# A two-layer decoder trunk: the residual stream kept with channels on the partitions from the first output projection on

## The chip, the cores and the metric

The kernel runs on one core of a Trainium2 chip. The metric is the time of one execution on the device in microseconds (us). The engines are TensorE (PE: matrix products; PEld: its weight loads), VectorE (DVE), ScalarE (ACT), GpSimd (POOL) and SyncE (SP, which issues nearly all DMAs here). Each engine works through its own instructions in order; semaphores tie the engines together.

## The reference

The input x has 512 tokens of 1024 channels. Two layers follow each other. The attention branches are not touched by the change, and stand here as one call each.

```python
for i in range(2):
    h = rms_norm(x, norm_gain[i])                    # over the 1024 channels
    y = (even_layer, odd_layer)[i](h, ...)           # h @ w_in, four kinds of attention, gates, then @ w_out
    x = x + y
    gate = sigmoid(rms_norm(x, ple_norm_gain[i]) @ w_ple_gate[i])
    x = x + (p[i] @ w_ple_proj[i]) * gate            # per-layer embedding
return x
```

`even_layer` has indexer-selected attention and a sliding window, `odd_layer` dilated and differential attention. Both end in `concat(...) @ w_out`, 1024 x 1024.

## The kernel before

**Products.** Everything is float32. Each operand of a projection is split into a rounded part and a rest (`hilo`: ScalarE writes the rounded part, VectorE subtracts), and a product is made of three passes (`PASSES`) of 128 x 128 x 512. `AT` holds the activations of the running projection with channels on the partitions: 8 channel tiles of 128 channels x 512 tokens, both parts. `w2` tiles (eight buffers) hold the split weights. `proj_tok` (L406) makes a token-major result: a 128-token slice of `AT` is the stationary operand, 512 columns of weights are streamed, and each of the four token tiles fills a PSUM bank (`mm_bank`, four of them). With order "kt" the weight tiles are the outer loop and all banks finish together; with "tok" one token tile is finished after the other. `proj_gate` (L441) does it the other way: 128 columns of weights stand still, 512 tokens are streamed, and the result has channels on the partitions. The trace writes the streamed operand first: `mm<-w,AT` is `proj_tok`, `mm<-AT,w` is `proj_gate`.

**The residual stream.** `X` is two tiles, one for each half of the channels, with 128 tokens on the partitions and 4 token tiles x 512 channels along them. `reload_x` (L740) brings x back before the output projection. `out_half` (L729) multiplies one branch's half of the concatenation by `w_out`, first for the lower 512 output channels ("kt"), then for the upper 512 ("kt" or "tok"); `add_x` adds a bank to `X`. `norm` (L510) then takes the four token tiles: `turn` transposes 4 blocks of 128 x 128 on TensorE for each half and splits them into `AT` (`swap` puts the lower half's channels in the upper half of `AT`, since the other half is still read); `norm_scale` sums the squares of a token by ScalarE's accumulator, adds the two halves on VectorE and takes the power -0.5 on GpSimd, one column per token tile. The scale of the norm is applied after the projection, as a number per partition (per token). `ple` (L744) is the gate of the per-layer embedding: two halves of 512 channels, each `proj_tok` with order "tok" and 96 products; `evac` applies tanh with the scale on ScalarE, and two VectorE steps build the new `X`, which is written to `out` or to `xkept`. In the very last half the last token tile is made in two pieces of 256 columns (`cut`). `ple_products` (L707) makes the product of p and `w_ple_proj` ahead of time. Three norms use `turn`: those of the two embeddings and that of layer 1. `scale_rows` (L494) makes the scales available along the free dimension, for `proj_gate`, by two DMAs through DRAM.

**The order.** The program records all instructions with an estimated duration, and `Program.order` plays them through a list scheduler: on each engine the ready instruction with the lowest rank goes next, the rank being its place in the program less a lead from the table `LEADS`, one entry for each call of a marked function. The resulting order of each engine is fixed. In the trace every instruction has line L278, where they are issued, so that groups are told apart by their tiles (`sk` is the bank that `turn` fills, `tk` that of the heads' and probabilities' turns).

Of the kernel before, what the change touches and what calls it, by code (L numbers as in the profile page):

```python
# [21 lines left out]
P = 128  # L22
# [9 lines left out]
    "att": (-392, -476, -265, 55, 575, -382, 44, 15, -6, -149, -341, -446, -4, -57, 63, -14, 2, 2, -287, 388, 0, 0,  # L32
# [7 lines left out]
    "idx": (-5, -2, 0),  # L40
    "mm": (15, 0, 153, 0, 10, -336, -84, 2, 8, 4, 0, -30, 30, -5, 88, -12, -304, 0, 41, 13, 136, -25, 206, -141, -135,
         -6, -996, -1930, -2303, -10383),
    "norm": (-3, -2, 0, -170, 60, -38, 0, -13, 142, 15, 0, -227, 0, -49, 15, -1, 0, 0, -396, -7, 21, 0, 0, -1844),
    "rows": (0, 898),
    "ss": (-64, 0, 0, 340, 576, 4, -39, 1269, 0, 0, -74, 119, 196, 55, 333, 112, -4, 45, -250, -182, 70, 0, 0, 1, 14,
         -119, 0, 74, 0, 1, 0, -88),
    "tab": (279, 13, -4, 0, -137, -2),
    "top": (193, -101, -908, -1349, 180, 58, -8, -21, -2, 3, -1659, -1846),
    "w": (-57, 169, 413, -21, 0, -44, -172, 0, 3, 0, -2, 1, -44, 74, -2, -20, -89, 234, 3, 68, -363, 0, 0, -80, -19,
         0, -19, 0, -854, -1336),  # L50
    "x": (2, 0),
    "y": (825, 483, 0, -2, -20, 0, 0, -16, 32, 4, 0, 202, 1, -123, -517, -335),
    None: 62,
# [26 lines left out]
class Program:  # L80
# [49 lines left out]
    def _price(self, engine, method, reads, writes):  # L130
# [22 lines left out]
        return 218 / 128 * n  # L153
# [128 lines left out]
def tile_trunk(ctx: ExitStack, tc: tile.TileContext, a: dict, out: bass.AP):  # L282
# [122 lines left out]
    @nc.part("mm")  # L405
    def proj_tok(pieces_n, evac, tiles=range(NT), order="kt", act=None, swap=0, cut=False, first=False):  # L406
        pieces, n = pieces_n
        act = [AT[:, :, kt, :] for kt in range(NK)] if act is None else act
        banks = {}
        last = len(pieces) - 1  # L410

        def mms(t, i, c0=0, c1=n, passes=range(3)):
            kt, w2 = pieces[i]
            for c in passes:
                xa, wa = PASSES[c]
                nc.tensor.matmul(banks[t][:, c0:c1], act[kt ^ (4 * swap)][:, xa, t * P:(t + 1) * P], w2[:, wa, c0:c1],
                                 start=(i == 0 and c == 0), stop=(i == last and c == 2))
        if order == "kt":
# [12 lines left out]
        else:  # L431
            for t in tiles:
                halves = ((0, 256), (256, 512)) if cut and t == NT - 1 else ((0, n),)
                for c0, c1 in halves:
                    banks[t] = mm_bank()
                    for i in range(last + 1):
                        mms(t, i, c0, c1)
                    evacuate(evac, t, banks[t], *((c0, c1) if cut else ()))

    @nc.part("mm")  # L440
    def proj_gate(pieces_n, y0, done, rsb):  # L441
# [3 lines left out]
        for i, (kt, w2) in enumerate(pieces):  # L445
            for m in range(4):
                for c, (xa, wa) in enumerate(PASSES):
                    nc.tensor.matmul(banks[m], w2[:, wa, m * P:(m + 1) * P], AT[:, xa, kt, :],
# [34 lines left out]
    def norm_scale(t, rs, times=1.0):  # L483
# [5 lines left out]
        if times != 1.0:  # L489
            nc.vector.tensor_scalar(out=e, in0=e, scalar1=times ** -2, scalar2=None, op0=ALU.mult)  # L490
# [11 lines left out]
    def turn(t, half, to):  # L502
        b = s_bank()
        for i in range(4):
            nc.tensor.transpose(b[:, i * P:(i + 1) * P], X[half][:, t, i * P:(i + 1) * P], ident)
        hs = slice(to * 4, to * 4 + 4)
        bv = b.rearrange("p (k n) -> p k n", k=4)
        hilo(AT[:, 0, hs, t * P:(t + 1) * P], AT[:, 1, hs, t * P:(t + 1) * P], bv)

    def norm(times=1.0, swap=0):  # L510
        rs = sb.tile([P, NT], F32, name=uid("rsn"), tag="rsn", bufs=2)
        for t in range(NT):
            for half in range(2):
                turn(t, half, half ^ swap)
            norm_scale(t, rs, times)
        return rs
# [190 lines left out]
    def ple_products(layer, homes=None):  # L707
        pT, _ = weights([(a["pT"][layer], T)], range(2))
        halves = []
        for c in range(2):  # L710
# [10 lines left out]
            proj_tok(weights([(a["w_ple_proj"][layer][:, c * 512:(c + 1) * 512], 512)], range(2)), evac,  # L721
                     act=[w2 for _, w2 in pT])
# [6 lines left out]
    def out_half(wout, y0, order):  # L729
        for c in range(2):  # L730
# [4 lines left out]
            proj_tok(w, add_x(c), order="kt" if c == 0 else order)  # L735
# [8 lines left out]
    def ple(layer, pws, rs, last, swap):  # L744
        for c in range(2):
# [6 lines left out]
            def evac(t, bank, c0=0, c1=512, c=c, pw=pw):  # L752
                th = tmp()[:, c0:c1]
                nc.scalar.activation(out=th, in_=bank[:, c0:c1], func=AF.Tanh, scale=rs[:, t:t + 1])
# [4 lines left out]
                nc.sync.dma_start(out=out[0, t * P:(t + 1) * P, c * 512 + c0:c * 512 + c1] if last else xkept[c][:, t, :], in_=xs)  # L759
            proj_tok(w, evac, order="tok", swap=swap, cut=last and c == 1)  # L760
# [190 lines left out]
    proj_tok(weights(ocols("ck"), range(NK), 2), head_evac(ckT, (tab_ck[:, 0], tab_ck[:, 1]), rs1), order="tok")  # L951
# [11 lines left out]
    proj_tok(weights(ocols("cv"), range(NK), 2), cv_evac)  # L963
# [78 lines left out]
    rows1 = scale_rows(rs1)  # L1042
# [4 lines left out]
    proj_tok(wcq, head_evac(cqT, (tab_cq[:, 0], tab_cq[:, 1]), rs1))  # L1047
# [3 lines left out]
    proj_gate(wdg, 4, 0, rows1)  # L1051
# [4 lines left out]
    proj_tok(wdk, head_evac(dkT, (tab_dk[:, 0], tab_dk[:, 1]), rs1))  # L1056
    wdq = weights(ocols("dq"), range(NK), 2)
    dqT = heads()
    proj_tok(wdq, head_evac(dqT, (tab_dq[:, 0], tab_dq[:, 1]), rs1))
    dV = slot([P, NT, 512])  # L1060
    proj_tok(weights(ocols("dv"), range(NK), 2), dv_evac)
# [4 lines left out]
    proj_gate(wcg, 0, 4, rows1)  # L1066
# [6 lines left out]
    ple(1, pw1, norm(0.5), True, 0)  # L1073
# [56 lines left out]
```

## Time and profile before

| | |
|---|---|
| median of three timed runs | 676.76 us (676.32 to 677.66) |
| the profiled execution | 677.39 us |
| its span from first to last instruction | 675.6 us |
| TensorE busy | 668.0 us, 3494 products |
| VectorE, ScalarE, GpSimd busy | 513.7, 415.4, 68.7 us |

All numbers of the profile are of the one profiled execution. The busy time of an engine counts each moment once, but the matrix products overlap each other, so that the mean time of one is longer than the distance from one to the next. Each digit of a line of tenths is a fortieth of the span, here 16.9 us.

### The profile page before, as it was taken

What the parts mean: (1) busy time and instruction counts of PE and PEld (TensorE: products, weight loads), DVE (VectorE), ACT (ScalarE), POOL (GpSimd) and SP (SyncE); (2) the same over time, 40 slices, a digit from 0 to 9 for tenths busy, and PEclk for the clock granted to TensorE, in tenths of its full rate; (3) what the DMA queues carried; (4) which work ended last, traced back from release to release, by engine and by line L of the source; (5) the groups of instructions that cost most, each with busy time, mean ns of one, the idle gap of its engine ahead of it and who ended that gap; (6) DMA issues with size and microseconds to landing.
All of it is one profiled execution on the core that took longest, in us unless ns stands there. A gap on an engine that the chain in (4) does not pass through costs nothing.

```text
span 675.6 us, 10378 instructions
## 1 busy us (share of the span) xinstructions
PE 668.0 (99%) x3494; PEld 543.9 (81%) x3494; DVE 513.7 (76%) x1225; ACT 415.4 (61%) x957; POOL 68.7 (10%) x55
## 2 busy tenths in 40 slices
PE   8999999999999999999999999999999999999997
PEld 5888888888988888887778877777887777888886
DVE  6699999999999646464795298989869698655443
ACT  6765678999889725355554365766637476564341
POOL 0120132000100000000230040003031000100100
PEclk9999999999999999999999999999999999999999
DMA  9855146653131521253353322123213034132222
GB/s 333 299 144 153 63 126 168 183 148 141 48 111 49 185 79 54 71 183 101 87 156 99 94 62 79 48 63 94 86 40 97 29 114 136 48 111 63 93 79 78
DMA packets 49621, 74.23 MB, mean 110 GB/s; under 512 B 5920, under 2 KB 18592, under 8 KB 49312
## 3 DMA queue, kind: packets, MB, share of 16 engines
q1 hardware_dynamic: 49424, 73.56, 35.3%
q8 instruction: 27, 0.44, 0.3%
q14 instruction: 26, 0.21, 0.1%
q10 hardware_dynamic: 144, 0.02, 0.0%
HBM read 61.49 MB, written 6.30 MB: 100 GB/s over the span
## 4 chain that ended last, share of the span: by engine, by line
PE 92%; DMA 3%; DVE 2%; ACT 1%; issue 1%; SPq 0%; DVEq 0%; ACTq 0%
PE mm L278 70%; PE sk L278 8%; PE ob L278 7%; PE tk L278 6%; DMA raw<-in_w_in_odd_dram 2%; DMA slot<-in_xT_dram 1%; DVE t L278 1%; DMA raw<-in_w_out_odd_dram 1%; DVE w L278 1%; ACT w L278 0%; DVE AT L278 0%; ACT t L278 0%; DVE slot L278 0%; SPq L278 0%; DVE tiny L278 0%
## 5 line engine op out<-in xcount | busy, mean ns | idle before, releaser
L278 PE MATMUL mm<-w,AT 128*128 128x512 f32 (+2 forms) x1728 | 433.6, 397 | 1.2 <-ACT w L278 0.6
L278 PEld LDWEIGHTS mm<-w,AT 128*128 128x128 f32 x1728 | 313.4, 188 | 69.6 <-issue 1.6
L278 PE MATMUL mm<-AT,w 128*128 128x512 f32 x384 | 104.9, 404 | 0.0
L278 ACT ACTIVATE w<-raw,gains 128x512 fp32r<-128x512 f32 x96 | 67.7, 722 | 58.8 <-PE mm L278 51.5
L278 DVE SCALAR_TENSOR_TENSOR w<-raw,gains,w 128x512 fp32r<-128x512 f32 x96 | 69.9, 746 | 39.1 <-ACT w L278 38.7
L278 POOL TENSOR_TENSOR tiny<-tiny,mhalf 128x8 f32<-128x8 f32 (+1 forms) x32 | 56.9, 1780 | 351.2 <-DVE tiny L278 351.2
L278 PEld LDWEIGHTS mm<-AT,w 128*128 128x128 f32 x384 | 68.6, 189 | 12.9 <-issue 1.1
L278 ACT ACTIVATE pr<-pr,nm 128x256 f32<-128x256 f32 (+3 forms) x128 | 68.6, 539 | 11.6 <-DVE nm L278 11.3
L278 PE MATMUL sk<-slot,slot 128*128 128x256 f32 (+7 forms) x368 | 64.6, 330 | 0.0
L278 DVE TENSOR_TENSOR w<-raw,w 128x512 fp32r<-128x512 f32 x80 | 53.8, 682 | 14.0 <-ACT w L278 13.6
L278 ACT CAST w<-raw 128x512 fp32r<-128x512 f32 x79 | 47.6, 620 | 22.2 <-PE mm L278 13.4
L278 PEld LDWEIGHTS sk<-slot,slot 64*128 64x128 f32 (+1 forms) x368 | 43.9, 187 | 12.0 <-issue 3.8
L278 PE MATMUL tk<-ident,pr 128*128 128x128 f32 x256 | 43.7, 275 | 0.0
L278 DVE SCALAR_TENSOR_TENSOR t<-t,slot 128x512 f32<-128x512 f32 (+1 forms) x17 | 11.2, 659 | 35.0 <-ACT t L278 35.0
L278 PEld LDWEIGHTS ob<-pt,Ve 128*128 128x128 f32 x272 | 35.1, 191 | 2.7 <-ACT pt L278 1.2
L278 PE MATMUL ob<-pt,Ve 128*128 128x128 f32 x272 | 37.2, 276 | 0.0
L278 PEld LDWEIGHTS tk<-ident,pr 128*128 128x128 f32 x256 | 31.2, 141 | 7.0 <-ACT pt L278 1.5
L278 ACT ACTIVATE t<-mm,rsn 128x512 f32<-128x512 f32 (+1 forms) x17 | 11.0, 662 | 40.0 <-PE mm L278 40.0
L278 DVE TENSOR_TENSOR t<-raww,tab 128x512 f32<-128x512 f32 x48 | 32.4, 684 | 4.0 <-ACT raww L278 3.9
L278 DVE CUSTOM_DVE_ANT_0 pr<-sk,cpack 128x128 f32<-128x128 f32 (+3 forms) x72 | 31.1, 461 | 5.6 <-PE sk L278 5.5
L278 ACT COPY pt<-tk 128x512 f32<-128x512 f32 (+3 forms) x56 | 27.4, 489 | 12.1 <-PE tk L278 8.6
L278 POOL TENSOR_TENSOR rsn<-tiny,mhalf 128x1 f32<-128x1 f32 x16 | 11.3, 710 | 215.6 <-DVE tiny L278 215.5
(100 smaller groups left out, 797.1 us busy)
## 6 DMA issues: line engine op xcount, KB each, us to landing
raw<-in_w_in_odd_dram SPq DMA_DIRECT2D x64, 256.0 KB, 2.8
raw<-in_w_in_even_dram SPq DMA_DIRECT2D x36, 256.0 KB, 3.0
raw<-in_w_ple_gate_dram SPq DMA_DIRECT2D x32, 256.0 KB, 2.6
slot<-in_x_dram SPq DMA_DIRECT2D x16, 256.0 KB, 6.6
raw<-in_w_out_even_dram SPq DMA_DIRECT2D x16, 256.0 KB, 2.8
raw<-in_w_out_odd_dram SPq DMA_DIRECT2D x16, 256.0 KB, 2.6
slot<-qh SPq DMA_DIRECT2D x22, 128.0 KB, 2.4
slot<-ql SPq DMA_DIRECT2D x22, 128.0 KB, 2.5
```

What stands on the lines that cost most here:

```text
L278: getattr(getattr(nc, engine), method)(*args, **kw)
```

## The change

From the output projection of layer 0 to the end, `X` holds channel tiles: 128 channels on the partitions, 512 tokens along them; its tile k is `X[k // 4][:, k % 4, :]`.

- `reload_x` reads the transposed x, which was already an input. The output is written transposed and turned back on the host after the run.
- `proj_tok` gets `flip`: the weights stand still, the activations are streamed, and each bank is a channel tile. The output projections, the embedding's gates and `ple_products` use it.
- `norm` has no transposes: `split_x` splits a channel tile straight into `AT`, `add_squares` squares a tile on ScalarE and adds it to a sum on VectorE, and `column_scales` sums over the partitions by four small products with a column of -0.5, scales on VectorE and takes one power of four columns. `scale_rows` now turns the four columns of scales on TensorE and copies the bank; all four norms use it, layer 0 too.
- In `ple` the scale varies along the free dimension, so a VectorE multiplication by the rows stands ahead of the tanh.
- A new order "mix" makes the first four weight tiles for all banks and then the last four bank by bank. The gates of `ple` and the first projection of layer 1 (`ck`) use it. Layer 1 keeps its `AT` halves swapped.
- The order table `LEADS` has new numbers throughout (left out here), and the planner's price of a small float32 product is raised to that of 128 columns.

```diff
@@ proj_tok @@
-                nc.tensor.matmul(banks[t][:, c0:c1], act[kt ^ (4 * swap)][:, xa, t * P:(t + 1) * P], w2[:, wa, c0:c1],
-                                 start=(i == 0 and c == 0), stop=(i == last and c == 2))
+                x2, mine = act[kt ^ (4 * swap)], slice(t * P, (t + 1) * P)
+                if flip:
+                    nc.tensor.matmul(banks[t][:, c0:c1], w2[:, wa, mine], x2[:, xa, c0:c1],
+                                     start=(i == 0 and c == 0), stop=(i == last and c == 2))
+                else:
+                    nc.tensor.matmul(banks[t][:, c0:c1], x2[:, xa, mine], w2[:, wa, c0:c1],
+                                     start=(i == 0 and c == 0), stop=(i == last and c == 2))
...
+        elif order == "mix":
+            early = [t for t in tiles if not (cut and t == NT - 1)]
+            for t in early:
+                banks[t] = mm_bank()
+            for i in range(4):
+                for t in early:
+                    mms(t, i)
+            for t in early:
+                for i in range(4, last + 1):
+                    mms(t, i)
+                evacuate(evac, t, banks[t])
+            if cut:
+                for c0, c1 in ((0, 256), (256, 512)):
+                    banks[NT - 1] = mm_bank()
+                    for i in range(last + 1):
+                        mms(NT - 1, i, c0, c1)
+                    evacuate(evac, NT - 1, banks[NT - 1], c0, c1)
@@ scale_rows, norm @@
     def scale_rows(rs):
+        b = t_bank()
+        for t in range(NT):
+            nc.tensor.transpose(b[:, t * P:(t + 1) * P], rs[:, t:t + 1].to_broadcast([P, P]), ident)
         rows = sb.tile([P, T], F32, name=uid("rows"), tag="rows", bufs=1)
-        line = dram.tile([NT, P], F32, name=uid("line"), tag=uid("line"), bufs=1)
-        nc.sync.dma_start(out=line.rearrange("t p -> p t"), in_=rs)
-        nc.sync.dma_start(out=rows, in_=line.rearrange("t p -> (t p)").partition_broadcast(P))
+        nc.scalar.copy(out=rows, in_=b)
         return rows
...
-    def turn(t, half, to):
-        b = s_bank()
-        for i in range(4):
-            nc.tensor.transpose(b[:, i * P:(i + 1) * P], X[half][:, t, i * P:(i + 1) * P], ident)
-        hs = slice(to * 4, to * 4 + 4)
-        bv = b.rearrange("p (k n) -> p k n", k=4)
-        hilo(AT[:, 0, hs, t * P:(t + 1) * P], AT[:, 1, hs, t * P:(t + 1) * P], bv)
+    def split_x(k, to):
+        hilo(AT[:, 0, to, :], AT[:, 1, to, :], X[k // 4][:, k % 4, :])
+
+    @nc.part("ss")
+    def add_squares(acc, k):
+        sq = acc if k == 0 else tmp()
+        nc.scalar.activation(out=sq, in_=X[k // 4][:, k % 4, :], func=AF.Square, scale=1.0 / 32.0)
+        if k:
+            nc.vector.tensor_tensor(out=acc, in0=acc, in1=sq, op=ALU.add)
+
+    @nc.part("rs")
+    def column_scales(acc, times):
+        b = t_bank()
+        for t in range(NT):
+            nc.tensor.matmul(b[:, t:t + 1], acc[:, t * P:(t + 1) * P], mhalf[:, :1], start=True, stop=True)
+        e = tiny(4)
+        nc.vector.tensor_scalar(out=e, in0=b[:, :NT], scalar1=-2.0 * times ** -2, scalar2=EPS * times ** -2,
+                                op0=ALU.mult, op1=ALU.add)
+        rs = sb.tile([P, NT], F32, name=uid("rsn"), tag="rsn", bufs=2)
+        nc.gpsimd.tensor_tensor(out=rs, in0=e, in1=mhalf[:, :NT], op=ALU.pow)
+        return rs
 
     def norm(times=1.0, swap=0):
-        rs = sb.tile([P, NT], F32, name=uid("rsn"), tag="rsn", bufs=2)
-        for t in range(NT):
-            for half in range(2):
-                turn(t, half, half ^ swap)
-            norm_scale(t, rs, times)
-        return rs
+        acc = sb.tile([P, T], F32, name=uid("qh"), tag="qh", bufs=QB)
+        for k in range(NK):
+            split_x(k, k ^ (4 * swap))
+            add_squares(acc, k)
+        rs = column_scales(acc, times)
+        return rs, scale_rows(rs)
@@ ple @@
-                nc.scalar.activation(out=th, in_=bank[:, c0:c1], func=AF.Tanh, scale=rs[:, t:t + 1])
+                nc.vector.tensor_tensor(out=th, in0=bank[:, c0:c1], in1=rows[:, c0:c1], op=ALU.mult)
+                nc.scalar.activation(out=th, in_=th, func=AF.Tanh)
...
-            proj_tok(w, evac, order="tok", swap=swap, cut=last and c == 1)
+            proj_tok(w, evac, order="mix", swap=swap, cut=last and c == 1, flip=True)
@@ tile_trunk @@
-    reload_x(x_in)
+    reload_x(lambda t, c: a["xT"][(4 * c + t) * P:(4 * c + t + 1) * P, :])
...
-    ple(0, pw0, norm(0.5, 1), False, 1)
-    rs1 = norm()
+    ple(0, pw0, norm(0.5, 1)[1], False, 1)
+    rs1, rows1 = norm(1.0, 1)
...
-    ple(1, pw1, norm(0.5), True, 0)
+    ple(1, pw1, norm(0.5)[1], True, 0)
```

## Rows read from the trace of the kernel before

**Rows 1.** The page, parts 1 and 2: busy time, tenths of the span, granted clock.

```profile
PE 668.0 (99%) x3494; PEld 543.9 (81%) x3494; DVE 513.7 (76%) x1225; ACT 415.4 (61%) x957; POOL 68.7 (10%) x55
...
PE   8999999999999999999999999999999999999997
...
PEclk9999999999999999999999999999999999999999
```

**Rows 2.** The page, part 4: the chain that ended last, by engine.

```profile
PE 92%; DMA 3%; DVE 2%; ACT 1%; issue 1%; SPq 0%; DVEq 0%; ACTq 0%
```

**Rows 3.** TensorE's waits, whole span: us in total, times, longest; first and last of five.

```profile
PE ob L278 <- DVE zeros L278: 1.2, 1, 1.2
...
PE sk L278 <- DVE AT L278: 0.2, 1, 0.2
```

**Rows 4.** The chain from 586 us to the end: start us, us, what, times.

```profile
586.41 0.90 PE ob L278 x8
...
614.03 2.80 PE mm L278 x12
616.83 0.44 PE sk L278 x4
617.27 2.80 PE mm L278 x12
...
627.38 43.98 PE mm L278 x213
...
671.38 0.48 ACT t L278
```

**Rows 5.** Busy time by stretch: layer 1's first projection, last norm, half a gate.

```profile
core 0: us, PE busy (x) PEld busy (x) DVE busy (x) ACT busy (x) POOL busy (x), PEclk, DMA share, GB/s
...
327.00:350.00 23.00, 22.89 (x109) 18.27 (x108) 17.42 (x32) 12.81 (x24) 6.90 (x4) 1.00 0.32 84
...
600.00:627.00 27.00, 27.00 (x133) 22.08 (x132) 15.57 (x27) 14.58 (x30) 0.87 (x2) 1.00 0.27 84
627.00:649.00 22.00, 22.00 (x98) 17.69 (x97) 9.06 (x17) 7.36 (x15) 1.75 (x3) 1.00 0.26 88
```

**Rows 6.** TensorE's groups by shape: the turns of x; busy us, mean ns.

```profile
L278 PE MATMUL sk<-ident,slot 128*128 128x128 f32 x96 | 17.8, 272 | 0.2 <-DVE AT L278 0.2
```

**Rows 7.** The chain from 195 to 300 us: layer 0's last gate, output projection, turns.

```profile
200.03 6.43 PE mm L278 x28
...
234.25 23.09 PE mm L278 x99
257.34 0.44 PE sk L278 x4
...
290.26 0.87 PE sk L278 x8
```

**Rows 8.** The page, part 5: weight loads of float32 products of 128 columns.

```profile
L278 PEld LDWEIGHTS ob<-pt,Ve 128*128 128x128 f32 x272 | 35.1, 191 | 2.7 <-ACT pt L278 1.2
```

**Rows 9.** VectorE's groups by shape, four of them.

```profile
L278 DVE SCALAR_TENSOR_TENSOR w<-raw,gains,w 128x512 fp32r<-128x512 f32 x96 | 69.9, 746 | 39.1 <-ACT w L278 38.7
...
L278 DVE TENSOR_TENSOR t<-t,t 128x512 f32<-128x512 f32 x27 | 18.4, 683 | 0.0
...
L278 DVE TENSOR_TENSOR t<-mm,rows 128x512 f32<-128x512 f32 x16 | 11.0, 685 | 4.6 <-PE mm L278 4.6
...
L278 DVE TENSOR_TENSOR t<-raww,slot 128x256 f32<-128x256 f32 x8 | 3.2, 413 | 0.0
```

**Rows 10.** ScalarE's groups by shape: a copy from PSUM, squares, reads of the accumulator.

```profile
L278 ACT ACTIVATE t<-slot 128x512 f32<-128x512 f32 x32 | 19.9, 624 | 7.6 <-DVE slot L278 7.6
...
L278 ACT COPY pt<-tk 128x512 f32<-128x512 f32 x28 | 16.2, 580 | 4.2 <-PE ob L278 2.2 <-PE tk L278 1.8
...
L278 ACT ACTIVATION_READ_ACCUMULATOR t<-slot 128x1 f32 x32 | 6.1, 190 | 0.0
```

**Rows 11.** GpSimd's groups by shape: powers of eight, one and four columns.

```profile
L278 POOL TENSOR_TENSOR tiny<-tiny,mhalf 128x8 f32<-128x8 f32 x24 | 47.4, 1978 | 260.4 <-DVE tiny L278 260.4
L278 POOL TENSOR_TENSOR rsn<-tiny,mhalf 128x1 f32<-128x1 f32 x16 | 11.3, 710 | 215.6 <-DVE tiny L278 215.5
L278 POOL TENSOR_TENSOR tiny<-tiny,mhalf 128x4 f32<-128x4 f32 x8 | 9.5, 1186 | 90.9 <-DVE tiny L278 90.9
```

More of the change, by code (lines that the diff above doesn't have):

```diff
@@ L31 @@
 LEADS = {
-    "att": (-392, -476, -265, 55, 575, -382, 44, 15, -6, -149, -341, -446, -4, -57, 63, -14, 2, 2, -287, 388, 0, 0,
[7 rows of a table removed]
[L40 to L53, printed above, removed]
+    "att": (0, 0, -81, 45, 612, -130, 0, 140, 17, -458, 0, 0, 38, 193, 0, -10, -9, -61, -119, -221, 13, 0, -115, -23,
[6 rows of a table added]
+    "idx": (0, 51, 0),
+    "mm": (-97, -11, -6, 9, 0, -60, -91, 43, 45, 0, 0, 0, 44, 106, 197, 150, 29, 317, 0, -62, 90, -28, 206, -110,
+         -144, 21, -89, -128, -62, -827),
+    "norm": (432, 0, -204, -38, 560, -164, 0, 1466, 58, 333, 23, -37, -7, 22, 1960, -44, 0, 11, 0, 183, -8, 20, 0,
+         -45),
+    "rows": (-790, -83, -204, -158),
+    "rs": (-46, 68, -131),
+    "ss": (761, 23, 302, 0, 426, 397, 22, 12, -237, 0, 237, 1, 0, -42, 0, 12, -218, 2, 0, 21, -42, 11, -87, -117, 21,
+         318, 20, 283, -142, 40, 0, -21),
+    "tab": (81, 9, 686, -145, -571, -371),
+    "top": (239, -200, -555, -632, -8, 0, -12, -197, -13, -172, -336, -759),
+    "w": (-4, -399, -61, -40, -47, -15, 0, 0, 0, -9, -2, 0, -154, 0, -83, 9, -57, -243, 0, -41, -11, 0, -44, 2, 6,
+         106, 17, -104, -461, -544),
+    "x": (230, 209),
+    "y": (-966, 7, 17, -548, -143, -51, 0, -27, -250, 0, -263, -194, 67, 13, 88, 108),
+    None: 61,
 }
@@ L405, in proj_tok @@
     @nc.part("mm")
-    def proj_tok(pieces_n, evac, tiles=range(NT), order="kt", act=None, swap=0, cut=False, first=False):
+    def proj_tok(pieces_n, evac, tiles=range(NT), order="kt", act=None, swap=0, cut=False, first=False, flip=False):
         pieces, n = pieces_n
@@ L430, in proj_tok, with proj_gate @@
                 evacuate(evac, t, banks[t])
+        elif order == "mix":
[15 more added lines that the diff above has]
+                    evacuate(evac, NT - 1, banks[NT - 1], c0, c1)
         else:
             for t in tiles:
[L433 to L438, printed above, removed]
+                banks[t] = mm_bank()
+                for i in range(last + 1):
+                    mms(t, i)
+                evacuate(evac, t, banks[t])
     @nc.part("mm")
-    def proj_gate(pieces_n, y0, done, rsb):
+    def proj_gate(pieces_n, y0, done, rsb, swap=0):
         pieces, n = pieces_n
@@ L447, in proj_gate @@
                 for c, (xa, wa) in enumerate(PASSES):
-                    nc.tensor.matmul(banks[m], w2[:, wa, m * P:(m + 1) * P], AT[:, xa, kt, :],
+                    nc.tensor.matmul(banks[m], w2[:, wa, m * P:(m + 1) * P], AT[:, xa, kt ^ (4 * swap), :],
                                      start=(i == 0 and c == 0), stop=(i == last and c == 2))
@@ L734, in out_half @@
                     split_y(m)
-            proj_tok(w, add_x(c), order="kt" if c == 0 else order)
+            proj_tok(w, add_x(c), order="kt" if c == 0 else order, flip=True)
     xkept = [dram.tile([P, NT, 512], F32, name=f"xkept{c}", tag=f"xkept{c}", bufs=1) for c in range(2)]
@@ L742, in reload_x, with ple @@
         load_x(range(NT), src)
-    def ple(layer, pws, rs, last, swap):
+    def ple(layer, pws, rows, last, swap):
         for c in range(2):
@@ L758, in evac @@
                 nc.vector.scalar_tensor_tensor(out=xs, in0=th, scalar=0.5, in1=xs, op0=ALU.mult, op1=ALU.add)
-                nc.sync.dma_start(out=out[0, t * P:(t + 1) * P, c * 512 + c0:c * 512 + c1] if last else xkept[c][:, t, :], in_=xs)
-            proj_tok(w, evac, order="tok", swap=swap, cut=last and c == 1)
+                k = 4 * c + t
+                nc.sync.dma_start(out=out[k * P:(k + 1) * P, c0:c1] if last else xkept[c][:, t, :], in_=xs)
+            proj_tok(w, evac, order="mix", swap=swap, cut=last and c == 1, flip=True)
     def causal(qb):
@@ L950, in tile_trunk @@
     ckT = heads()
-    proj_tok(weights(ocols("ck"), range(NK), 2), head_evac(ckT, (tab_ck[:, 0], tab_ck[:, 1]), rs1), order="tok")
+    proj_tok(weights(ocols("ck"), range(NK), 2), head_evac(ckT, (tab_ck[:, 0], tab_ck[:, 1]), rs1), order="mix", swap=1)
     rs1h = const.tile([P, NT], F32, name="rs1h")
@@ L961, in dv_evac @@
         nc.scalar.activation(out=dV[:, t, :], in_=bank, func=AF.Copy, scale=rs1[:, t:t + 1])
-    proj_tok(weights(ocols("cv"), range(NK), 2), cv_evac)
+    proj_tok(weights(ocols("cv"), range(NK), 2), cv_evac, swap=1)
     @nc.part("att")
@@ L1055, in tile_trunk @@
     dkT = heads()
-    proj_tok(wdk, head_evac(dkT, (tab_dk[:, 0], tab_dk[:, 1]), rs1))
+    proj_tok(wdk, head_evac(dkT, (tab_dk[:, 0], tab_dk[:, 1]), rs1), swap=1)
     wdq = weights(ocols("dq"), range(NK), 2)
     dqT = heads()
-    proj_tok(wdq, head_evac(dqT, (tab_dq[:, 0], tab_dq[:, 1]), rs1))
+    proj_tok(wdq, head_evac(dqT, (tab_dq[:, 0], tab_dq[:, 1]), rs1), swap=1)
     dV = slot([P, NT, 512])
-    proj_tok(weights(ocols("dv"), range(NK), 2), dv_evac)
+    proj_tok(weights(ocols("dv"), range(NK), 2), dv_evac, swap=1)
     wcg = weights(ocols("cg"), range(NK), 2)
@@ L1124 @@
         aps[name] = nc.dram_tensor(f"in_{name}_dram", arr.shape, mybir.dt.from_np(arr.dtype), kind="ExternalInput").ap()
-    out = nc.dram_tensor("out_0_dram", (1, T, D), F32, kind="ExternalOutput").ap()
+    out = nc.dram_tensor("out_0_dram", (D, T), F32, kind="ExternalOutput").ap()
     with tile.TileContext(nc) as tc:
```

17 lines of the change are left out of this document (7 added, 10 removed), and 13 rows, old and new, of the table LEADS.

## Prediction

> **What bounds the kernel now.** I read the page first [rows 1]. TensorE's row says 99% of the span, its line of tenths is 9 from the second slice to the last but one, and the granted clock is 9 in every slice, that is, the upper of the two levels (2.4 GHz) with nothing to win back. VectorE has 76% and is full only in layer 0. A busy matrix engine alone proves little, since its records overlap, so I went on to the chain of waits: 92% of the span is TensorE's own instructions one behind the other [rows 2]. The list of waits of TensorE holds five single waits, 3.2 us in all; the first and the last of them are shown [rows 3]. Last I read the chain piece by piece around a norm [rows 4]: twelve products, four turns of x, twelve products, without a gap. So what sets the end is the sum of what TensorE has to do, at its pace, and an instruction removed from it is time removed, so long as no new wait appears. The load of the other engines around the norms says whether they can follow [rows 5]: VectorE is busy 0.41 to 0.76 of those stretches, ScalarE 0.33 to 0.56.
>
> **Part 1, the turns of x go.** Each of the three norms turned X with 4 tiles x 2 halves x 4 = 32 transposes, 96 in all; the group is there with x96 [rows 6]. Its mean, 272 ns, is the time from start to end and not what one costs in a stream. The cost is read from the chain: four in 0.44 us, both at 257.34 and at 616.83 us, and eight in 0.87 us at 290.26, so 0.109 each [rows 4, 7]. 96 x 0.109 = **-10.5 us**. This lies on the path in full, since nothing else runs on TensorE meanwhile. TensorE: Matmul & The Clock Gate (the Trainium skill, Part 4, PE-mode transpose) gives about 275 ns for one 128x128 transpose inside a kernel. By that 96 of them would be worth 26.4 us; it is near the 272 ns of the row, but the chain shows that four finish in 0.44 us, so here the page's figure is a latency. I take 0.109; the other price is a rival below.
>
> **Part 2, the products are turned round.** The output projections (2 x 192) and the gates of the embedding (2 x 192), 768 products of 512 columns, now hold the weights still and stream the activations; their number and size stay. The head-group gates already do it that way (the group moves AT over w). In the chain 28 of those take 6.43 us, 0.2296 each; 99 of an output projection in the old form take 23.09 us, 0.2332 each [rows 7]. 768 x 0.0036 = **-2.8 us**, with 0 as the other end if the difference comes from the place of the gates and not from the operands. The 96 of the embedding products swap two operands of the same kind: nothing.
>
> **Part 3, what TensorE gets back.** Norms: 12 products with one moving column. A plain float32 product runs as two instructions (272 rows of ob<-pt,Ve for 136 calls of the program), so 24 instructions. No row shows one column. From below: the last run of the kernel, 165 products of 512 columns and 48 of 256, takes 43.98 us; less 165 x 0.2333 this leaves 0.114 for 256 columns, about half of 0.233, so by columns alone one column would cost nearly nothing. From above: the weight load, 0.191 us, if it is not hidden [rows 4, 8]. Between them is the spacing of float32 products of 128 columns, eight in 0.90 us, 0.112 each [rows 4]; like the turns, they come no closer than one load of 128 columns can follow another, and I take that: 24 x 0.11 = **+2.6 us** (0 to 4.6). Rows of scales: four calls (layer 0 gets it too) x 4 turns of a broadcast column = 16, at 0.109 **+1.75 us**, up to 16 x 0.191 = 3.1 if the broadcast load is slow.
>
> **Part 4, the other engines.** Per norm VectorE adds seven sums of 512 at 0.683; per embedding eight multiplications by the rows at 0.685, since the scale no longer is a number per partition [rows 9]: 4.8 + 5.5 = 10.3 us in a norm and its gate, which in layer 1 take 49 us with 24.6 us of VectorE's work [rows 5]. That makes 0.71, and it is hidden; without that cover each 512-wide step costs 0.68. ScalarE squares as before (0.624), but the 24 reads of its accumulator at 0.190 go (-4.6 us) and four copies of rows at 0.58 come [rows 10]. GpSimd: per norm one power of four columns, 1.186, for four of one column, 0.710 [rows 11]. Each scale_rows loses two DMAs on SP's queue; the queue gets shorter and nothing on it waited for them. reload_x and the writes of out and xkept have the same number and bytes.
>
> **Part 5, the joins.** Before, a gate product needed only its own token tile turned, so norm and gate ran tile by tile. Now every gate product needs all tokens of a channel tile. What covers it is the "mix" order: 4 weight tiles x 4 banks x 3 passes = 48 products on the half of X that was finished first, 48 x 0.233 = 11.2 us, while the second half is added (0.68), rounded by ScalarE and subtracted by VectorE (0.58 and 0.68) [rows 9, 10]. One tile's chain is 2.0 us; the last addition, four tiles and four weight tiles on VectorE are 0.68 + 4 x 0.68 + 4 x 0.75 = 6.4 us. It fits. AT's half for the new values is free in time, because the old half is read only in the first 48 products of the previous gate. The row of scales is first needed when bank 0 is to be used again, 96 products = 22.4 us after the join; VectorE has 6.4 + 8 x 0.68 = 12 us of work after the join at the most, then products 0.9, power 1.19, turns 0.44 and copy 0.58: some 15 us. Behind the small products and the turns of scales everything on TensorE queues, so a wrong place costs at once. Before, one of the three norms has a visible hold-up (a turn waits until AT's last bank is read, 0.2 [rows 3]). I set the same 0.2 for the new waits, net 0.
>
> **Part 6, the end.** The last 256 columns pass a multiplication (0.413, the nearest row is another 256-wide one, plus 0.05 of handing on) before the tanh at 671.38 us: **+0.46 us**, bare [rows 4, 9].
>
> **Sum.** -10.5 - 2.8 + 2.6 + 1.75 + 0.46 = **-8.5 us**. The profiled run took 677.39 us with a span of 675.6; the median of the three timed runs is 676.76. The span should be 667.1, a profiled run 668.9, the median **668.3 us**. With every bound at its good end (-10.5 - 2.8 - 0.2 + 0 + 1.75 + 0.46) it is -11.3, 665.5 us; with every one at its bad end (-10.5 + 0 + 4.6 + 3.1 + 0.46) it is -2.3, 674.4 us.
>
> **Rivals.** (a) New waits at the joins eat most of it. The four banks of "mix" are wanted within 9 products, 2.1 us, of the last product before, and VectorE has to empty the last one in that time at 0.68 plus its backlog; five such joins (four gates and the first projection of layer 1) with 1 us each give 5 us back, 673.3, and with more up to 675.4 us. For it: VectorE at 0.76 after the first embedding [rows 5]. Against: five waits in the whole kernel before, which is full of such joins [rows 3]. (b) TensorE is busy but paced by others, so that the turns are merely replaced by waiting: 676.8 us. Perfetto Trace Analysis (the Trainium skill, Identifying the Most-Contended Engine) says that matmul busy time is a poor measure and that the weight loads' share is the better one; that share is 81% here [rows 1]. By that rule up to a fifth of the time would be slack; the even spacing of 0.233 in the chain speaks against it, no other engine being near full at the norms. (c) Slower: in each norm TensorE's in-order queue meets the small products and the turns of the scales before their data. With nothing between, the chain square 0.62, add 0.68, products 0.9, power 1.19, turns 0.44, copy 0.58 is bare [rows 9 to 11]; less TensorE's own 1.3 it is 3.1 us a norm, and with a backlog of two steps on VectorE 4.5. Three norms give 9.3 to 13.5 us: 678 to 682 us. It decides once the wait per norm passes (8.5 + 1.35) / 3 = 3.3 us. Against: the turns of the heads hang on a power of 1.98 us and never hold TensorE up [rows 3, 11]. (d) More gain: the turns cost their latency [rows 6], -96 x 0.272 against +40 x 0.272 for the new small ones: -26.1 + 10.9 + 0.46 - 2.8 = -17.5, 659.3 us; or the retuned order also removes hold-ups elsewhere, 662 to 664.
>
> **How the numbers follow.** Forecast, between the bounds but for the last 2 us of the bad end (665.5 to 672.4): 0.68. Rival (a), 672.4 to 675.4: 0.13. (b), within 0.2% (1.35 us, about what a measurement can tell from no change): 0.06. (c): 0.06. (d): 0.07, of it 0.02 for the latency price. Faster by over 0.2% is forecast, (a) and (d): 0.88; within 0.06; slower 0.06. For 8 in 10 the range takes the forecast, two thirds of (a) and half of (d): 663.8 to 674.4 us.
>
> **What would show it.** Right: the group of x96 gone and 24 + 16 small ones in its place, at about 0.11 each in the chain; 0.230 instead of 0.233 in the output projections; still a handful of waits; VectorE in the norms near 0.75. Wrong: waits of TensorE on VectorE or GpSimd at the three norms (c), on VectorE at the start of a "mix" (a), or products spaced further apart than 0.233 with no wait named (b).

## The result and the profile after

| | before | after |
|---|---|---|
| median of the timed runs | 676.54 us (676.32 to 677.66) | 665.86 us (665.33 to 666.99) |
| ratio of the two, 95% interval | | 0.9841 (0.9823 to 0.9859) |
| the profiled execution, its span | 677.39, 675.6 us | 665.33, 663.5 us |
| forecast | | 668.3 us (663.8 to 674.4) |

The change makes the kernel 10.7 us faster; a second comparison on another occasion gave 0.9853 (0.9838 to 0.9868), 675.67 against 665.49 us, which is 10.2 us. Forecast were 8.5.

The page after, part 1 (busy time), the line of tenths of VectorE, and part 4 (the chain), to be read beside [rows 1, 2]:

```profile
PE 657.9 (99%) x3438; PEld 539.6 (81%) x3438; DVE 530.9 (80%) x1246; ACT 415.1 (63%) x937; POOL 66.9 (10%) x46
...
DVE  6699999999998647559777389888998889458465
...
PE 99%; DVE 0%; ACT 0%; issue 0%
```

TensorE still sets the end, now with 99% of the chain where 92% was its share before, and it has 56 instructions fewer: 96 turns gone, 16 turns and 24 products come. VectorE has 17 us more. The list of TensorE's waits has shrunk from five [rows 3] to one, the start:

```profile
PE ob L279 <- DVE zeros L279: 1.2, 1, 1.2
```

TensorE's groups by shape; `sk<-ident,slot` [rows 6] is no longer there, the last two groups are new:

```profile
L279 PE MATMUL mm<-AT,w 128*128 128x512 f32 x1128 | 282.2, 399 | 0.0
L279 PE MATMUL mm<-w,AT 128*128 128x512 f32 x840 | 220.6, 403 | 0.0
...
L279 PE MATMUL tk<-mhalf,qh 128*128 128x1 f32 x24 | 3.3, 208 | 0.0
L279 PE MATMUL tk<-ident,rsn 128*128 128x128 f32 x16 | 3.0, 272 | 0.0
```

The chain from 230 to 330 us (start us, us, what) covers layer 0's output projection, gates and the next norm, as [rows 7] did:

```profile
235.47 43.73 PE mm L279 x191
279.32 0.34 PE mm L279
279.77 0.34 PE mm L279
...
286.99 0.33 PE tk L279 x3
287.32 0.23 PE mm L279
287.66 38.60 PE mm L279 x167
```

and its last run of products, 103 of 512 columns and 48 of 256:

```profile
629.82 29.25 PE mm L279 x151
```

191 products without a break take 0.2290 us each; the same stretch before ran at 0.2332 and was broken by turns. The column sums come in pairs of instructions between two products: from one of these products to the next it is 0.45 (279.32, 279.77, 280.23) where a product alone takes 0.23, so a pair costs 0.22, 0.11 an instruction. Three of the turns of scales take 0.33, 0.11 each.

Busy time by stretch after, in the second half of layer 0's gate and layer 1's norm behind it (290 to 328) and in layer 1's last projection and first half gate (590 to 620); columns as in [rows 5]:

```profile
290.00:313.00 23.00, 23.00 (x102) 18.76 (x101) 21.30 (x34) 13.91 (x25) 0.00 (x0) 1.00 0.50 160
313.00:328.00 15.00, 15.00 (x70) 12.20 (x69) 12.41 (x21) 8.29 (x14) 0.00 (x0) 1.00 0.55 172
...
590.00:620.00 30.00, 30.00 (x132) 24.61 (x132) 22.73 (x38) 18.69 (x33) 0.00 (x0) 1.00 0.31 92
```

TensorE is full in all of them, but VectorE is at 0.93 in the first, where the prediction had counted on 0.71 from layer 1.

### The profile page after: what moved, and what is told of

It is laid out like the page before. It is cut to its first block, busy times and chain, and to the rows that moved or that the text cites. A ratio compares the mean times of both kernels' runs of the same rounds, so it can differ in the third digit from the quotient of the medians.

```text
span 663.5 us, 10249 instructions
## 1 busy us (share of the span) xinstructions
PE 657.9 (99%) x3438; PEld 539.6 (81%) x3438; DVE 530.9 (80%) x1246; ACT 415.1 (63%) x937; POOL 66.9 (10%) x46
## 4 chain that ended last, share of the span: by engine, by line
PE 99%; DVE 0%; ACT 0%; issue 0%
PE mm L279 77%; PE ob L279 9%; PE tk L279 7%; PE sk L279 7%; DVE t L279 0%; ACT t L279 0%; DVE slot L279 0%; DVE zeros L279 0%
## 5 line engine op out<-in xcount | busy, mean ns | idle before, releaser
L279 PE MATMUL mm<-AT,w 128*128 128x512 f32 (+1 forms) x1176 | 287.8, 394 | 0.0
L279 PEld LDWEIGHTS mm<-AT,w 128*128 128x128 f32 x1176 | 212.4, 188 | 42.9 <-issue 0.6
L279 PE MATMUL mm<-w,AT 128*128 128x512 f32 (+1 forms) x936 | 239.4, 400 | 0.0
L279 PEld LDWEIGHTS mm<-w,AT 128*128 128x128 f32 x936 | 171.3, 189 | 35.0 <-issue 0.9
L279 PE MATMUL sk<-slot,slot 128*128 128x256 f32 (+7 forms) x368 | 60.6, 332 | 0.0
L279 PEld LDWEIGHTS sk<-slot,slot 64*128 64x128 f32 (+1 forms) x368 | 41.8, 187 | 13.5 <-issue 4.2
L279 DVE TENSOR_TENSOR t<-mm,rows 128x512 f32<-128x512 f32 (+1 forms) x33 | 21.9, 671 | 18.7 <-ACT rows L279 10.9
L279 PEld LDWEIGHTS tk<-ident,pr 128*128 128x128 f32 x256 | 31.5, 140 | 5.7 <-ACT pt L279 0.8
L279 ACT ACTIVATE t<-t 128x512 f32<-128x512 f32 (+1 forms) x33 | 20.0, 614 | 24.6 <-DVE t L279 24.5
L279 POOL TENSOR_TENSOR rsn<-tiny,mhalf 128x1 f32<-128x1 f32 (+1 forms) x7 | 10.8, 1543 | 242.3 <-DVE tiny L279 242.2
```

The source lines that it names most:

```text
L279: getattr(getattr(nc, engine), method)(*args, **kw)
```

## The experiments

In what follows "the changed kernel" is at 665.5 to 665.9 us. Each run was timed beside the kernel before, and differences to the changed kernel are of medians; its two ratios above (0.984 and 0.985) say how far these can be trusted, about 1 us.

**The turns put back.** Theory: a turn costs its spacing in the chain. Rivals: its latency, or nothing.

```diff
     def split_x(k, to):
+        b, place, lead, nc.lead = s_bank(), nc.place, nc.lead, 0
+        for i in range(4):
+            nc.tensor.transpose(b[:, i * P:(i + 1) * P], X[k // 4][:, k % 4, i * P:(i + 1) * P], ident)
+        nc.place, nc.lead = place, lead
```

> The changed kernel with the 96 turns of x put back on TensorE (four transposes for each channel tile in each of the three norms, into a bank nobody reads; nothing else differs). Changed kernel: 665.9 us. Theory (a turn costs its spacing, 0.109 us, all of it on the path): +10.5, 676.4 us. Rival (it costs its latency, 0.272): +26, 692 us. Rival (TensorE is paced by other engines): no difference, 666 us.

Measured: 676.03 us, ratio 1.0002 (0.9993 to 1.001) to the kernel before: +10.2 to +10.5 us. The turns alone return all of the gain. The chain from 580 us on:

```profile
611.79 0.44 PE sk L279 x4
612.23 3.23 PE mm L279 x14
615.46 0.44 PE sk L279 x4
615.90 2.08 PE mm L279 x9
```

Four in 0.44 us again; the group `sk<-ident,slot` is back with x96 and a mean of 272 ns. Ninety-six at 272 would have been 26 us. TensorE has no wait but the first, so the turns cost their spacing, neither more nor less than the medians can tell.

**The products turned back.** Theory: the operands set the pace. Rival: the place in the kernel does.

```diff
-            proj_tok(w, add_x(c), order="kt" if c == 0 else order, flip=True)
+            proj_tok(w, add_x(c), order="kt" if c == 0 else order)
...
-            proj_tok(w, evac, order="mix", swap=swap, cut=last and c == 1, flip=True)
+            proj_tok(w, evac, order="mix", swap=swap, cut=last and c == 1)
```

> The changed kernel with the 768 products of the output projections and the embedding's gates the old way round: activations stand still, weights are streamed. What comes out of these products is then turned block by block and is not the reference's; their number, size and order stay. Theory (the operands set the pace, 0.2333 against 0.229): +3.2, 669.1 us, and the spacing in the chain is 0.233 again in these stretches. Rival (the pace belongs to the place in the kernel): no difference, spacing stays 0.229.

Measured: 668.42 us (ratio 0.9888, 0.9875 to 0.99), +2.6 to +2.9. The chain in the same place as above:

```profile
235.48 44.57 PE mm L279 x191
```

44.57 / 191 = 0.2333 against 0.2290. The place is the same, only the operands have changed places; so the pace belongs to the operands. What about them makes 4 ns was not tried.

**The column sums made four times.**

```diff
+            for _ in range(4):
-            nc.tensor.matmul(b[:, t:t + 1], acc[:, t * P:(t + 1) * P], mhalf[:, :1], start=True, stop=True)
+                nc.tensor.matmul(b[:, t:t + 1], acc[:, t * P:(t + 1) * P], mhalf[:, :1], start=True, stop=True)
```

> The changed kernel with each of the 12 column-sum products made four times over, 72 instructions more. Theory (one costs the spacing of two loads of 128 columns, 0.112 an instruction): +8.1, 674.0 us. Rival (cost goes by the one column that is streamed): below +0.5, 666.3 us. Rival (the weight load is bare, 0.19): +13.7, 679.6 us.

Measured: 675.11 us (0.9985, 0.9974 to 0.9995), +9.2 to +9.6, between two expectations. That a column costs next to nothing is refuted. The trace tells the rest. TensorE's groups in time and the busy time by stretch, around layer 1's norm:

```profile
328.37 3.09 PE L279 MATMUL tk<-mhalf,qh 128*128 128x1 f32 x26
331.32 0.78 PE L279 MATMUL mm<-w,AT 128*128 128x512 f32 x1
...
333.88 6.49 PE L279 MATMUL mm<-w,AT 128*128 128x512 f32 x19
```

```profile
326.00:333.00 7.00, 7.00 (x43) 6.31 (x42) 1.44 (x3) 1.34 (x2) 0.00 (x0) 0.86 0.45 149
333.00:339.00 6.00, 6.00 (x18) 4.85 (x19) 2.91 (x7) 1.32 (x2) 1.23 (x2) 0.59 0.00 0
339.00:345.00 6.00, 6.00 (x27) 4.82 (x26) 2.67 (x6) 4.12 (x7) 1.98 (x2) 1.00 0.13 41
```

Twenty-six one-column instructions in a row take 3.09 us; from one start to the next it is 0.112, but for the last two. Behind them the granted clock falls from 1.00 to 0.59 for some 6 us although TensorE was never idle; 19 products take 6.49 us where 19 x 0.233 + 0.25 = 4.7 is their pace, and three lone ones before take 0.77 where such a product takes 0.48 in the changed kernel. So 72 x 0.112 = 8.1 us is the instructions, and 2 to 3 us of this execution the clock at its lower level (1.2 GHz). The eleven timed runs bear the split out: the one whose mean granted clock was 1.000 took 673.86 us, +8.0 to +8.4, and the five at 0.994 or 0.993 took 676.1 to 676.8.

**Order "tok" in place of "mix" in layer 0's gates.** Theory: "mix" covers the join. Rival: the new values are there in time anyway.

```diff
...
-            proj_tok(w, evac, order="mix", swap=swap, cut=last and c == 1, flip=True)
+            proj_tok(w, evac, order="mix" if last else "tok", swap=swap, cut=last and c == 1, flip=True)
```

The part left out gives "tok" back its two pieces of 256 columns, which layer 0 does not use.

> The changed kernel with order tok in place of mix in the two gates of layer 0's embedding; everything else stays. Theory (mix is what covers the join: 48 products, 11.2 us, against 12 products, 2.8 us, while VectorE has 6.4 us to do; and the half of AT for layer 1's norm comes free only at the end of the gates): TensorE waits some 3.5 us at the first join and 1.5 at the second, +5, 671 us. Rival (the order of the banks does not matter, the new values are there in time anyway): no difference, 666 us.

Measured: 673.75 us (0.9967, 0.9952 to 0.9981), +7.9 to +8.3. TensorE's groups in time, its waits (us in total, times, longest), and the stretch after the wait that ends at 298.30:

```profile
261.74 15.84 PE L279 MATMUL mm<-AT,w 128*128 128x512 f32 x68
...
287.76 8.61 PE L279 MATMUL mm<-AT,w 128*128 128x512 f32 x35 [1.50 <-ACT w L279]
298.30 19.49 PE L279 MATMUL mm<-AT,w 128*128 128x512 f32 x77 [1.93 <-ACT w L279]
317.62 0.86 PE L279 MATMUL mm<-w,AT 128*128 128x512 f32 x3
320.21 0.50 PE L279 MATMUL mm<-w,AT 128*128 128x512 f32 x1 [1.73 <-DVE t L279]
```

```profile
PE mm L279 <- ACT w L279: 3.4, 2, 1.9
PE mm L279 <- DVE t L279: 1.7, 1, 1.7
PE ob L279 <- DVE zeros L279: 1.2, 1, 1.2
PE mm L279 <- DVE w L279: 1.2, 2, 0.8
```

```profile
299.00:304.00 5.00, 5.00 (x17) 3.93 (x16) 3.15 (x6) 1.65 (x3) 0.00 (x0) 0.66 0.66 216
```

The new waits come to 5.9 us (another 0.4 of the list, at 10.60 us, is in the head), near the 5 expected, but more than half of them are not where they were expected. At the first join, where the last addition to `X` is at 267 us, TensorE has no wait at all up to 286 us; the 3.5 us foreseen there did not come. The two waits of 3.4 us in total before 287.76 and 298.30 are for weights (`ACT w`), in the second half of the gate. With "tok" all eight buffers of `w2` stay in use until the last bank, and ScalarE, which copies the row of scales and takes two tanh first, splits the weights of the second half only from 287.0 us on; with "mix" four come free early, and in the changed kernel it splits three of the new tiles at 272.38, 275.12 and 277.87. Only the 1.73 and the 0.76 at layer 1's norm are the second join, 2.5 us for the 1.5 foreseen. After the 1.93 the granted clock is 0.66 over the next 5 us, some 1.7 us more. So with this order table "mix" in layer 0 is worth three quarters of the gain. The table was made for "mix"; what one made for "tok" would hide was not tried.

**Rows of scales by DMA.** Theory: 22 us are enough to hide them. Rival: they come late.

```diff
-        b = t_bank()
-        for t in range(NT):
-            nc.tensor.transpose(b[:, t * P:(t + 1) * P], rs[:, t:t + 1].to_broadcast([P, P]), ident)
         rows = sb.tile([P, T], F32, name=uid("rows"), tag="rows", bufs=1)
-        nc.scalar.copy(out=rows, in_=b)
+        line = dram.tile([NT, P], F32, name=uid("line"), tag=uid("line"), bufs=1)
+        nc.sync.dma_start(out=line.rearrange("t p -> p t"), in_=rs)
+        nc.sync.dma_start(out=rows, in_=line.rearrange("t p -> (t p)").partition_broadcast(P))
```

> The changed kernel with the rows of scales made as before, by two DMAs through DRAM, in all four places: 16 turns and four copies go. Theory (a turn costs 0.109 and the rows are needed only some 22 us after the join, so that the DMAs are hidden): -1.75, 664.1 us. Rival (the DMAs queue behind weights and come late, the banks are not emptied in time): TensorE waits on VectorE in the embedding's gates, +3 us or more.

Measured: 679.27 us (1.0059, 1.0038 to 1.0081), +13.4 to +13.8: slower than the kernel before. My theory falls here. TensorE's waits, then around the first embedding the instructions in time, the two DMAs (KB, us from issue to landing) and the stretches:

```profile
PE mm L279 <- DVE t L279: 12.1, 2, 9.2
```

```profile
282.19 0.38 SPq L279 DMA_DIRECT2D line<-rsn  x1
288.81 2.36 SPq L279 DMA_DIRECT2D raw<-in_w_in_odd_dram  x4
292.83 0.33 SPq L279 DMA_DIRECT2D rows<-line  x1
297.64 1.89 DVE L279 TENSOR_TENSOR t<-mm,rows 128x512 f32<-128x512 f32 x3 [6.82 <-DMA rows<-line]
```

```profile
rows<-line SPq DMA_DIRECT2D x1, 256.0 KB, 4.8
line<-rsn SPq DMA_DIRECT2D x1, 2.0 KB, 10.6
```

```profile
289.00:299.00 10.00, 0.78 (x3) 0.50 (x2) 3.18 (x6) 1.65 (x4) 0.00 (x0) 0.70 0.46 131
299.00:304.00 5.00, 5.00 (x14) 3.86 (x13) 4.90 (x9) 2.46 (x4) 0.00 (x0) 0.57 0.25 91
304.00:309.00 5.00, 5.00 (x23) 4.12 (x22) 2.85 (x5) 2.73 (x5) 0.00 (x0) 1.00 0.04 14
```

The first DMA, of 2 KB, is issued at 282.19 and takes 10.6 us to land. SP's queue waits for that landing before it issues the second at 292.83 (1.6 us by its list of waits, after four loads of weights that it has issued meanwhile), and the second lands near 297.6. So the two transfers alone take 15.4 us, and the theory had put them at nothing. Until then no bank can be emptied, and TensorE stands for 9.2 us, then runs at the lower clock for some 5 us more (0.57). In layer 1's embedding the first DMA takes 9.2 us to land and TensorE waits 2.9. The run has 1.75 us less to do in all and loses 12.1 by waiting and some 2 by the clock. The room was the 22 us of the theory: the last addition to `X` ends at 267.3, and TensorE runs out of banks at 289.3. But the order places the column sums only at 279.25, which is right for turns and too late for these DMAs; whether an order made for the DMAs would hide them was not tried.

**The multiplication made twice.** Theory: VectorE's added work is hidden. Rival: VectorE is near to being the bound.

```diff
+                place = nc.place
                 nc.vector.tensor_tensor(out=th, in0=bank[:, c0:c1], in1=rows[:, c0:c1], op=ALU.mult)
+                nc.place = place
+                nc.vector.tensor_tensor(out=th, in0=bank[:, c0:c1], in1=rows[:, c0:c1], op=ALU.mult)
```

> The changed kernel with the multiplication by the rows made twice in every evacuation of the embedding's gates: 17 more VectorE steps, 11.4 us of VectorE work. Theory (hidden under TensorE but for the last one, of 256 columns): +0.45, 666.3 us. Rival (VectorE is close to being the bound at the joins, banks come free late): several us, up to +11, with TensorE waiting on VectorE.

Measured: 667.42 us (0.9879, 0.9864 to 0.9893), +1.6 to +1.9, neither theory. TensorE's waits and the stretch of the second join, layer 1's norm:

```profile
PE mm L279 <- DVE t L279: 1.0, 2, 0.6
```

```profile
313.00:328.00 15.00, 13.98 (x61) 10.71 (x60) 15.00 (x25) 9.03 (x17) 0.00 (x0) 1.00 0.38 134
```

VectorE is full from 313 to 328 us, and TensorE waits for it there. Of 11.4 us of added work some 9.7 are still hidden, 0.4 lies bare at the end and about 1.3 comes out before and at the second join. The change itself, with half that work, shows no wait, so there it was hidden; but not much more would have been.

**Without the order table.** The table of leads was made anew for the change, and the gain could be the table's. Both kernels with an empty one (`LEADS = {None: 0}`):

> The changed kernel with an empty order table: every instruction has its program place as its rank. Together with the next run it parts what the structure brings from what the new table brings. Theory (the gain is TensorE's work, 9 us by the terms): both flat kernels are slower than the tabled ones by tens of us, since TensorE waits, and the difference between them is about 9 us or a few us more. Rival (the gain is the retuned table): the two flat kernels are equal, or the changed one is slower.

> The kernel before with an empty order table, the partner of the run above. Theory: slower than the flat changed kernel by about 9 us. Rival: equal.

Measured: 711.32 us (ratio 1.0531 to the kernel before, 1.0515 to 1.0547) and 723.47 us (1.07, 1.0681 to 1.072). Without any table the change is worth 12.2 us, with the two tables 10.2 to 10.7. TensorE's named waits add up to much the same in both traces, 31.5 us in the changed kernel and 32.6 in the one before, and its busy time is 673.0 against 685.8 us. So the gain is there without the table, in TensorE's work and not in its waiting. Crossing the tables was not possible: each is an order for its own list of calls.

**The kernel before once more**, for a second trace.

> The kernel before once more, for a second trace. The first trace has hold-ups of TensorE in the head (0.6 and 0.4 us named), at 321, 348 and 554 us. Theory (those in the head are the landing of the first loads, which differs from run to run; those at 321, 348 and 554 us belong to the order and come back): the later three are there again within 0.2 us, about 2 us together by the spacing, the head's differ; 676.5 us. Rival (all are chance): they are elsewhere or gone.

Measured: 676.52 us, ratio 1.0008 (0.9991 to 1.0025). Its profiled execution has a span of 673.8 us, 1.8 less than the first. TensorE's waits and its groups in time:

```profile
...
PE ob L278 <- ACT pt L278: 0.5, 1, 0.5
PE sk L278 <- DVE AT L278: 0.3, 1, 0.3
PE mm L278 <- DVE w L278: 0.2, 1, 0.2
```

```profile
319.03 0.27 PE L278 MATMUL sk<-ident,slot 128*128 128x128 f32 x1
319.60 0.33 PE L278 MATMUL sk<-ident,slot 128*128 128x128 f32 x1 [0.30 <-DVE AT L278]
...
551.42 0.40 PE L278 MATMUL mm<-AT,w 128*128 128x512 f32 x1
552.30 0.71 PE L278 MATMUL ob<-slot,pt 128*128 128x128 f32 x4 [0.48 <-ACT pt L278]
```

The wait of a turn for AT is there again (0.3 against 0.2), so is the one of `ob` (0.5 against 0.8); by spacing they cost more than their names: from one turn to the next 0.57 us where 0.11 is usual, from a product to the next 0.88 where 0.11 to 0.23 is. Worked out from the ends of neighbouring products it is 0.52 and, a little later, 0.29 at 320, and 0.75 at 552.7 us, 1.6 together. The one at 348 is gone, and the head lost 0.4 where the first trace lost 1.6 (both read from the ends of neighbouring products). So two of my three came back, that of `ob` shorter (0.75 against 1.09 by the same reckoning); the head and the third hold-up differ from run to run.

**Two leaner versions.** The rows by DMA only where they are needed late, in layer 0's and in layer 1's norm:

```diff
-    def scale_rows(rs):
+    def scale_rows(rs, near=False):
+        if not near:
...
+            nc.sync.dma_start(out=line.rearrange("t p -> p t"), in_=rs)
+            nc.sync.dma_start(out=rows, in_=line.rearrange("t p -> (t p)").partition_broadcast(P))
+            nc.place += 3
+            return rows
...
-    rs1, rows1 = norm(1.0, 1)
+    rs1, rows1 = norm(1.0, 1, False)
```

> The changed kernel with the rows of scales by two DMAs where they are needed late (layer 0's norm and layer 1's norm), and turned on TensorE where they are needed at once (the two embeddings). Eight turns go. Theory (a turn costs its spacing; what made the run with DMAs everywhere slow was the two embeddings alone): -0.87, 665.0 us, no wait of TensorE. Rival (a late DMA holds the rows' only buffer or a gate): a wait of some us.

and besides the column sums as one instruction each, on a rounded sum:

```diff
-            nc.vector.tensor_tensor(out=acc, in0=acc, in1=sq, op=ALU.add)
+            nc.vector.tensor_tensor(out=accr if k == NK - 1 else acc, in0=acc, in1=sq, op=ALU.add)
...
-            nc.tensor.matmul(b[:, t:t + 1], acc[:, t * P:(t + 1) * P], mhalf[:, :1], start=True, stop=True)
+            nc.tensor.matmul(b[:, 2 * t:2 * t + 2], acc[:, t * P:(t + 1) * P], half2, start=True, stop=True)
```

> The run above, and the sum of squares written rounded, so that each of the 12 column sums is one instruction of two columns in place of two of one (the sums' parts are then rounded, the result stays within the reference's tolerance by an estimate of rounding over 128 parts). Theory (each instruction costs 0.112 whatever it streams): another -12 x 0.112 = -1.3, 663.7 us. Rival (the pair costs no more than its second half does, since the first load is hidden behind a product): no further difference, 665.0 us.

The changed kernel itself beside them:

> The changed kernel as it is, beside the two runs above, so that they can be compared on one chip: 665.9 us.

Measured: 664.83 us (0.9837, 0.9825 to 0.985), 664.41 us (0.9845, 0.9818 to 0.9872) and 665.49 us (0.9853, 0.9838 to 0.9868). The signs are as expected, -0.7 and -1.1 us, but the intervals overlap: neither is shown to beat the changed kernel. In the trace of the second the sums are one instruction each:

```profile
L279 PE MATMUL tk<-half,ql 128*128 128x2 f32 x12 | 2.0, 165 | 0.0
```

but its profiled span, 662.8 us, is that of the first; it has a wait of `sk` for ScalarE of 0.5 us in layer 0 that the first has at 0.2, and one of `tk` of 0.3 that the first does not have.

## Why the prediction was right, and where it was off

The direction, the mechanism and the range held: TensorE's sum of work sets the end, and what is taken from it is gained. The measured -10.2 to -10.7 lies near the good end of the bounds (-11.3), but not by that end's route: there the column sums were to cost nearly nothing, and they cost 2.7; what made up for it are hold-ups that the sum had put at nothing. So the forecast came out some 2 us too small, and that the time still fell within the sum's own bounds (665.5 us at the good end) is luck. Step by step:

- **Turns, -10.5.** Put back, they cost 10.2 to 10.5. The choice of the spacing over the latency was the one that mattered: an estimate from the figure of the Trainium skill (TensorE: Matmul & The Clock Gate, Part 4, about 275 ns) would have put the changed kernel at some 659 us. The run with the turns disagrees with it as a cost in a stream, and agrees with it as a latency (272 ns).
- **Products turned round, -2.8.** Right in size, 2.6 to 2.9 by the run that undid it, but two of its readings were off and cancel. The 28 products that gave 0.2296 held three of the old form (25 head-group gates from 199.79 us and 3 products of `proj_tok` from 205.61); without them the pace is 0.2292. After the change it is 0.2290, but for layer 0's second half gate with 0.2299 (107 such products and 60 of the old form in 38.60 us), 0.2292 on average: 744 x 0.0041 = 3.05. And the 48 pieces of 256 columns went the other way. In the last run of the chain after (29.25 us), 103 products of 512 columns leave 0.118 for one of 256, where the prediction had worked out 0.114 before: 0.2 back, and -2.9 by the trace.
- **Given back, +2.6 and +1.75.** Both right in size. A pair of one-column instructions takes 0.22 out of the stream, 12 of them 2.7; the 16 turns keep to 0.11.
- **VectorE's cover.** Hidden, as said, but the reason given was mis-sized: 0.71 was worked out from layer 1, and layer 0's second gate stands at 0.93 after the change. With twice the multiplications it no longer covers all.
- **The joins.** No wait, as said. With "tok" in layer 0 8 us go, but its run had no wait at the first join either, where 12 products of cover against 6.4 us of VectorE's work should have left 3.5 us; what "mix" brings there is that the weights come in time. The row of scales has the room that I gave it, and the order as it stands uses it up: the changed kernel's copy of the row ends at 288.29 us and the first bank is emptied from 288.32 on. Made by two DMAs of 15.4 us it is late by 9.2.
- **The end, +0.46.** The last multiplication takes 659.09 to 659.51, as sized; 0.2 of it came back because the last write landed sooner.
- **Waits, net 0.** This is the step that failed. I took the waits that the list names as the hold-ups there were, set 0.2 for 0.2, and so left out what the change removes beside its own work. In the second trace of before the hold-up of a turn at 320 us costs 0.8 by spacing, not 0.3, and one at 553 us 0.75; after the change both are gone, 1.6 us, in both traces of the changed kernel. That the turn's own went is clear, since there is no turn; that the other went is seen, and that the new table did it only argued.

With the second trace of before the sum closes: -10.5 - 2.9 + 1.75 + 2.7 + 0.2 - 1.6 = -10.35, and the spans differ by 673.8 - 663.5 = 10.3 us. The first trace of before was 1.8 us longer, most of it in the head.

Of the rivals, (b) falls with the turns put back. With it falls, for this kernel, its reading of the weight loads' share as slack; the Trainium skill (Perfetto Trace Analysis, Identifying the Most-Contended Engine) names that share, beside the rate of arithmetic, as a measure of headroom. Here it is 81% before and after, while 10 us went. (a) and (c) did not happen here; the runs with "tok" and with DMAs show what they look like when they do. Of (d) the second half did, in part: of the 1.6 us of hold-ups that went, 0.75 were elsewhere.

## What to carry to other kernels

When one engine's instructions fill the chain, cost an edit by the distance from one instruction to the next in the chain, never by the mean duration, and count hold-ups by that distance too. Changing the layout so that a reduction crosses what used to be independent tiles may need a loop order that works on the part that is ready; look for the one value that every evacuation waits for (here the row of scales), and count the landing of every transfer in its path, however small (here 10.6 us for 2 KB). A run that takes one piece out of a kernel with a hand-made order also shows what that order was made for. A margin of cover is read in the stretch where it is thinnest, not in the one that is easiest to read.

## What the runs showed of the hardware that was not expected

- The granted clock fell to its lower level without an idle TensorE: in the run with the column sums made four times it read 1.00 before 26 one-column instructions in 3.09 us and 0.59 over the 6 us from 333 us on, and 19 products took 6.49 us in place of 4.7.
- After a wait of 9.2 us (rows by DMA) and one of 1.9 ("tok") it read 0.57 and 0.66 over the next 5 us, and each of the two cost some 2 us more than it lasted. After the 2.9 us in layer 1 of the run by DMA it read 1.00.
- Which operand stands still changes the pace of a 512-column product: 0.2290 with the weights standing and the activations streamed, 0.2333 the other way, in the same stretch of the same kernel. Of 256 columns it was 0.118 and 0.114, the other way round.
- A float32 product that streams one column takes two instructions of 0.11 us, as much as a turn each.
- A DMA of 2 KB, the four columns of scales to DRAM, took 9.2 and 10.6 us from issue to landing in the two embeddings of the run by DMA; the 256 KB back took 4.4 and 4.8.
